# Hybrid attention and recurrence layer: query and key halves stored by 64 rows, the inverse written by lane group

## The chip, the cores and the metric

One core of a Trainium2 chip runs the whole layer as one program. The metric is the device time of one execution in microseconds (us). In what follows PE is TensorE (PEld its weight loads), DVE is VectorE, ACT is ScalarE, POOL is GpSimd and SP is SyncE, which in this program only issues DMAs. The core has 16 DMA engines, which all queues share. "Line 378" or L378 is a line of the kernel before.

## The reference

One layer of a diffusion backbone, for 1,024 latent tokens and 256 context tokens of width 1,024, in float32. One input projection feeds two groups of heads.

```
h = rmsnorm(x) * (1 + scale) + shift;  u = h @ w_in
q, k, v, g_a, u_b, g_b = split(u)
# A: 8 heads of differential attention (two softmaxes of 64 columns each, one subtracted
#    from the other); latent tokens get a 2-D rotary on q and k and also read 512 cached keys
o_a = rmsnorm((softmax(q1 k1) - lam * softmax(q2 k2)) v) * silu(g_a)
# B: 16 heads of a bidirectional RWKV-7 recurrence, state 64 x 64 per head and direction
S = S * w_t + (S @ -kk_t) b_t^T + v_t k_t^T;   y_t = S r_t
o_b = (groupnorm(y) + bonus) * silu(g_b)
x = x + gate * (concat(o_a, o_b) @ w_out);  y = rmsnorm(x)
```

Outputs are both token sets, the context tokens' keys and values, and the final states of the recurrence.

## The kernel before

The program has two phases. In **phase one** (to about 1,460 us) the input projection runs as a list of 66 blocks of 128 columns, each in three chunks of 512, 512 and 256 tokens (`chunk`, lines 336 to 338, PE). After each chunk ACT copies the result out of PSUM, and every block that is still in work (a Python generator in the list `active`) issues its next piece. So the pieces of several blocks are interleaved on the in-order queues of ACT, DVE, POOL and SP.

- `b_qk` (one block for the query, one for the key of each of the 8 attention heads) has the query or key of one head transposed, 128 rows by 1,280 tokens: rows 0 to 63 are the first half (m = 0), rows 64 to 127 the second. It applies the rotary, splits the result into a high part (`hi`, ACT, line 624 or 616) and a low part (left in `u`, DVE, line 625 or 617), and stores both to DRAM. For six of the heads `hi` is one buffer of 512 tokens that is used three times in a row; for the last two heads it is one of 1,280 tokens. The key's block does the same with 512 cached keys (`ch`, `ck`, lines 604 to 608). Everything is stored through SP.
- `b_k` prepares the recurrence of a pair of heads: decays (`z`, line 417), operands (DVE `ra`, `bk`; POOL `ta`, `bk`, lines 476 to 485), products (`pg`, line 451) masked by DVE into `km` (line 452), a single buffer that SP stores twice (`kt`, `bt`, lines 460 and 462).
- The last blocks of the list are those of heads 6 and 7 of attention. Their `u` tiles come from a pool of four buffers, so a new block's copy out of PSUM waits until an older block's store has read its buffer. Beside them POOL computes the first triangular inverse (`inverse`, lines 737 and 739: 31 pairs of multiply and add).

In **phase two** ("mix") the recurrence goes through 10 items (2 groups of heads, 5 token segments), each in 4 parts. Each part loads its operands (`load_part`), and two parts ahead `load_early` loads `Bt` and `Tb`; `Tb` is the part's share of the item's inverse, read back from the DRAM tile `td`. `prep` (line 806, `yb`) multiplies the two. Between the steps, attention (`sc`, `pb`, `pa`, `po`), the norms and the output projection are filled in by a credit count. POOL computes the inverse of a later item meanwhile and writes it to `td` through its own DMA queue (line 741); the next inverse begins with a memset of the same SBUF tile (`tt`, line 732).

The initial states of the recurrence are transposed by PE ahead of the first item (line 831) and written to DRAM; before and after do this in the same way.

The lines that say how the two layouts stand:

```
s["q"]: [H, HD, 2, 2, T]      # head, row of the half, high/low, half m, token
s["k"]: [H, 2, HD, 2, NK]     # head, high/low, row of the half, half m, token
dq = lambda v, c: (...).rearrange("r m t -> m r t")   # 2 x 64 x tokens, from 128 rows
td0 = dram.tile([CH, P, CH], F32)                     # t, lane, s
```

Of the kernel before, what the change touches and what calls it, by code (L numbers as in the profile page):

```python
# [10 lines left out]
F32 = mybir.dt.float32  # L11
# [7 lines left out]
P = 128  # L19
# [4 lines left out]
T = TL + TP  # L24
NT = T // P
PAST = 512
# [6 lines left out]
CH = 32  # L33
# [4 lines left out]
HN = 2  # L38
NF = NC // HN
NL = 4  # L40
# [43 lines left out]
def tile_kernel(ctx: ExitStack, tc: tile.TileContext, i: dict, o: dict, heads=H, phases=3):  # L84
    nc = tc.nc

    dram = ctx.enter_context(tc.tile_pool(name="dram", bufs=1, space=DRAM))
    kp = ctx.enter_context(tc.tile_pool(name="kp", bufs=1, reuse_waits="tile"))
    s = {}
# [19 lines left out]
    scratch("y", [heads // NL, T, 2, 2, NL // 2, P])  # L109
    scratch("acc", [T, D])  # L110
    gate_d = s["gate"]
    td0 = dram.tile([CH, P, CH], F32, tag="td0", name="td0")

    ident = kp.tile([P, P], F32, name="ident")
    nc.sync.dma_start(ident, i["ident"])
# [7 lines left out]
    with ExitStack() as p1:  # L123
# [5 lines left out]
        n = 0  # L129
# [4 lines left out]
        n = 128  # L134
# [37 lines left out]
        with ExitStack() as p0:  # L172
# [24 lines left out]
            for n, g in enumerate(WORD):  # L197
                t = sp.tile([P, KD, 256], F32, tag="wa", name=f"wa{g}", bufs=8)
# [143 lines left out]
        def ut(nm):  # L342
            return up.tile([P, UP], F32, tag="u", name=nm)

        def plain(u):
            def f(ps, n0, n):
                nc.scalar.copy(u[:, n0:n0 + n], ps)
            return f
# [28 lines left out]
        def spill(dst, t):  # L377
            nc.sync.dma_start(dst, t)  # L378
# [196 lines left out]
            spill(s[name][j * P:(j + 1) * P, :], g)  # L575

        def b_qk(which, h):
            dq = lambda v, c: (s["q"][h, :, v, :, c] if which == "q" else s["k"][h, v, :, :, c]).rearrange("r m t -> m r t")
            off = PAST if which == "k" else 0
            u = ut(f"u{which}{h}")  # L580
            yield plain(u)
            su = ut(f"su{which}{h}")
            for b in range(8):
                nc.sync.dma_start(su[16 * b:16 * b + 16, 0:TL], u[16 * (b ^ 1):16 * (b ^ 1) + 16, 0:TL])
            if which == "k":
                ck = ap.tile([P, PAST // P, P], F32, tag="w2", name=f"ck{h}")
                nc.sync.dma_start(ck, i["cache_k"][0, 0, :, h].rearrange("(t p) m d -> p t (m d)", p=P))
            yield
            yield
            nc.gpsimd.tensor_tensor(su[:, 0:TL], su[:, 0:TL], sinT, op=ALU.mult)  # L590
            nc.gpsimd.tensor_tensor(u[:, 0:TL], u[:, 0:TL], cosT, op=ALU.mult)
            if which == "k":
                pk = psm.tile([P, 512], F32, tag="psm", name=f"pk{h}")
                ko = ap.tile([P, 512], F32, tag="hi", name=f"ko{h}", bufs=1)
                for t in range(2):
                    nc.tensor.transpose(pk[:, t * P:(t + 1) * P], u[:, TL + t * P:TL + (t + 1) * P], ident)
                nc.scalar.copy(ko[:, 0:2 * P], pk[:, 0:2 * P])
                nc.sync.dma_start(o["new_k"][0, 0, :, h].rearrange("(t p) m d -> p t (m d)", p=P),
                                  ko[:, 0:2 * P].rearrange("p (t n) -> p t n", n=P))
                pt = psm.tile([P, 512], F32, tag="psm", name=f"pck{h}")  # L600
                for t in range(4):
                    nc.tensor.transpose(pt[:, t * P:(t + 1) * P], ck[:, t, :], ident)
                ch = ap.tile([P, 512], F32, tag="hi", name=f"ch{h}", bufs=1)
                nc.scalar.copy(ch.bitcast(F32R), pt)
                cv = ck.rearrange("p t n -> p (t n)")
                nc.vector.tensor_tensor(cv.bitcast(F32R), pt, ch, op=ALU.subtract)
                nc.sync.dma_start(dq(0, slice(0, PAST)), ch)
                nc.sync.dma_start(dq(1, slice(0, PAST)), cv)
            yield
            yield  # L610
            nc.vector.tensor_tensor(u[:, 0:TL], u[:, 0:TL], su[:, 0:TL], op=ALU.add)
            if h >= heads - 2:
                hi = up.tile([P, T], F32, tag="s", name=f"hi{which}{h}", bufs=3)
                for n0, n in CHUNKS:
                    c = slice(n0, n0 + n)
                    nc.scalar.copy(hi[:, c].bitcast(F32R), u[:, c])
                    nc.vector.tensor_tensor(u[:, c].bitcast(F32R), u[:, c], hi[:, c], op=ALU.subtract)
                yield
                spill(dq(0, slice(off, off + T)), hi)
                spill(dq(1, slice(off, off + T)), u[:, 0:T])  # L620
                return
            for n0, n in CHUNKS:
                hi = ap.tile([P, 512], F32, tag="hi", name=f"hi{which}{h}_{n0}", bufs=1)[:, :n]
                nc.scalar.copy(hi.bitcast(F32R), u[:, n0:n0 + n])
                nc.vector.tensor_tensor(u[:, n0:n0 + n].bitcast(F32R), u[:, n0:n0 + n], hi, op=ALU.subtract)
                spill(dq(0, slice(off + n0, off + n0 + n)), hi)
            spill(dq(1, slice(off, off + T)), u[:, 0:T])

        def b_va(h):
            u = ut(f"uv{h}")[:, 0:T]  # L630
# [33 lines left out]
        def b_inv():  # L664
            nw = heads * 10
            nc.sync.dma_start(s["wc"][:, 0:nw, :], wcs[:, 0:heads].rearrange("r p i d c -> r (p i d) c"))
            yield
            aw = rp.tile([P, T], F32, tag="td", name="aw0")[:, 0:CH * CH].rearrange("p (t y) -> p t y", y=CH)
            tt = rp.tile([P, T], F32, tag="ta", name="tt0")[:, 0:CH * CH].rearrange("p (t y) -> p t y", y=CH)
            tmp = rp.tile([P, T], F32, tag="kn", name="tmp0")  # L670
            for n, _ in enumerate(inverse(nc, s, td0, inv_rows(heads, 0), aw, tt, tmp)):
                if n % 8 == 0:
                    yield

        rk = lambda h: [(COL_R + h * P, b_r(h), f"r{h}"), (COL_KB + h * P, b_k(h), f"k{h}"),
                        (COL_VB + h * P, b_v(h), f"v{h}"), (COL_GB + h * P, b_gate("gb", h), f"gb{h}")]
        at = lambda h: [(COL_Q + h * P, b_qk("q", h), f"aq{h}"), (COL_K + h * P, b_qk("k", h), f"ak{h}"),
                        (COL_V + h * P, b_va(h), f"av{h}"), (COL_GA + h * P, b_gate("ga", h), f"ga{h}")]
        sr = [t for h in range(heads) for t in rk(h)]
# [5 lines left out]
        for n, t in enumerate(sr[3:]):  # L685
            m = round((n + 1) * (len(sa) - LAG) / (len(sr) - 3))
# [33 lines left out]
def inv_rows(heads, b):  # L720
    return [(NL * (b // 5) + x, b % 5 - 1) for x in range(NL)]


def inverse(nc, s, td, rows, aw, tt, tmp):
    n = 32 * len(rows)
    for x, (p, sg) in enumerate(rows):
        bt = s["bt"][p // NL, sg + 1, :, :, :, :, p % NL].rearrange("f h d t y -> (f h d) t y")
        for c in range(HN):
            nc.sync.dma_start(aw[NL * c + x:n:NL * HN], bt[:, :, c * P + 96:c * P + P])
    yield  # L730
    e = nc.gpsimd
    e.memset(tt[:n], 0.0)
    e.memset(tt.rearrange("p s t -> p (s t)")[:n, 0:CH * CH:CH + 1], 1.0)
    for t in range(CH - 1):
        j, w = t + 1, CH - 1 - t
        mv = tmp[:n, 0:j * w].rearrange("p (w j) -> p w j", w=w)
        e.tensor_tensor(mv, aw[:n, t, t + 1:CH].unsqueeze(2).broadcast_to([n, w, j]),  # L737
                        tt[:n, t:t + 1, 0:j].broadcast_to([n, w, j]), op=ALU.mult)
        e.tensor_tensor(tt[:n, t + 1:CH, 0:j], tt[:n, t + 1:CH, 0:j], mv, op=ALU.add)  # L739
        yield  # L740
    nc.gpsimd.dma_start(td[:, 0:n].rearrange("t u s -> u t s"), tt[:n])


def mix_phase(ctx, tc, i, o, s, ident, nhalf, dram, td0, neglam, subg, lnh, heads, psm):
    nc = tc.nc
# [38 lines left out]
    tds = {0: td0}  # L784
# [3 lines left out]
    def load_early(j):  # L788
        m, f = j // NF, j % NF
        p0, sg = items[m]  # L790
        Bt = cp.tile([P, NL, HN, P], F32, tag="Bt", name=f"Bt{j}")
        nc.sync.dma_start(Bt.rearrange("r x c y -> r (x c y)"),
                          s["bt"][p0 // NL, sg + 1, f].rearrange("h d r x y -> (h d r) (x y)"))
        Tb = cp.tile([P, HN, NL, CH], F32, tag="Tb", name=f"Tb{j}")
        src = tds[m].rearrange("t (f q u) s -> f q t (u s)", f=NF, q=4)
        nc.sync.dma_start(Tb.rearrange("t c x s -> t (c x s)"), src[f])
        early[j] = (Bt, Tb)

    def prep(j, w, pp, chain):
# [27 lines left out]
    for g in range(heads // NL):  # L827
        for d in range(2):
# [3 lines left out]
            c = 512 * (2 * g + d)  # L832
# [6 lines left out]
    for w in duos:  # L839
        yield  # L840
        pp = psm.tile([P, 512], F32, tag="psm", name=f"pp{w}")
        prep(0, w, pp, [])
        put(0, w, pp)
    load_early(1)
    yield True

# [11 lines left out]
    def invert(b):  # L858
        rows = inv_rows(heads, b)
        aw = wk.tile([P, CH, CH], F32, tag="aw", name=f"aw{b}")  # L860
        tt = wk.tile([P, CH, CH], F32, tag="tt", name=f"tt{b}")
        tmp = wk.tile([P, CH * CH // 4], F32, tag="tmp", name=f"tmp{b}")
        tds[b] = dram.tile([CH, P, CH], F32, tag=f"td{b % 2}", name=f"td{b}")
        yield from inverse(nc, s, tds[b], rows, aw, tt, tmp)

    bank = [psx.tile([P, 512], F32, name=f"bank{n}") for n in range(2)]
# [603 lines left out]
    for t in range(n_tick):  # L1470
        m, c = t // NC, t % NC
        p0, sg = items[m]
        j, k = t // HN, t % HN
# [120 lines left out]
```

## Time and profile before

| | |
|---|---|
| median of 3 runs | 2894.51 us (2891.80 to 2897.08) |
| the profiled execution | 2891.34 us, its span 2889.6 us |
| PE busy | 2402.2 us, 83% |
| DVE, ACT, POOL busy | 1424.4, 1218.8, 1120.2 us (49%, 42%, 39%) |
| DMA queue of SP | 510,000 packets, 429.24 MB, 59.1% of 16 engines' span |
| DMA queue of POOL | 1,840 packets, 5.49 MB, 1.0% |
| mean granted TensorE clock | 0.912 |

Busy times are those of the span. The span holds everything from the first to the last instruction; about 2 us of the execution lie around it. An engine's busy time says how much work it has, not that the end waits for it: what sets the end is read stage by stage, from which wait ends last there.

### The profile page before, as it was taken

Reading aid. Unit: us, or ns where it says so; the run is one execution under the profiler, and the core shown is the slowest. Engines: PE = TensorE matmul, PEld = TensorE weight load, DVE = VectorE, ACT = ScalarE, POOL = GpSimd, SP = SyncE. Lnnn points to the kernel's source line nnn. Section 1 sums busy time; section 2 is a strip of 40 time slices with the busy share of each in tenths; the row PEclk is TensorE's granted clock in tenths of the full one; section 3 lists DMA queues with packets and bytes.
Section 4 is the critical chain, followed back from the end, with each engine's and each line's share of the span. In section 5 each row is a group of like instructions: output and inputs, shape, how many; then the busy total and the mean of one; then the engine's idle time right before and its main releaser. Section 6 shows DMA issues by size and latency. Waiting matters only on the chain. (4 is left out here: it accounts for less than half of the span.)

```text
span 2889.6 us, 59844 instructions
## 1 busy us (share of the span) xinstructions
PE 2402.2 (83%) x23875; PEld 1931.3 (67%) x23875; DVE 1424.4 (49%) x2794; ACT 1218.8 (42%) x2518; POOL 1120.2 (39%) x1655
## 2 busy tenths in 40 slices
PE   6978779896887987986644689889989998998896
PEld 5766667775776866865543577767757767676674
DVE  5634353543534453542112467656665544446666
ACT  3323333332333332322113577756655656454343
POOL 4233243332333333332622667656662221105354
PEclk9998899997998999998877899999989999799898
DMA  7354545553543644554237988978687977857534
GB/s 235 99 131 105 157 115 134 141 128 98 148 118 94 158 111 125 143 124 122 73 93 187 194 192 195 201 146 186 144 191 182 232 169 177 195 162 211 165 129 164
DMA packets 512119, 438.55 MB, mean 152 GB/s; under 512 B 155719, under 2 KB 449779, under 8 KB 510496
## 3 DMA queue, kind: packets, MB, share of 16 engines
q1 hardware_dynamic: 510000, 429.24, 59.1%
q0 software_dynamic: 1840, 5.49, 1.0%
q8 instruction: 188, 3.08, 0.5%
q14 instruction: 91, 0.75, 0.1%
HBM read 259.22 MB, written 164.39 MB: 147 GB/s over the span
## 5 line engine op out<-in xcount | busy, mean ns | idle before, releaser
L1090 PE MATMUL sc<-ka,q 128*128 128x512 f32 (+1 forms) x832 | 297.5, 444 | 35.7 <-DVE pb L1093 19.3
L1093 DVE TENSOR_SCALAR_CACHE_REDUCE pb<-sc,mn 128x512 f32<-128x512 f32 x256 | 191.5, 748 | 131.3 <-PE sc L1090 116.7
L1098 ACT ACTIVATE pb<-pb,mn 128x1536 f32<-128x1536 f32 (+1 forms) x160 | 218.2, 1364 | 80.9 <-DVE pb L1093 79.4
L1135 PE MATMUL po<-vk,aT 128*128 128x128 f32 x1600 | 244.6, 291 | 6.0 <-ACT aT L1122 5.9
L458 ACT COPY km<-ptk 64x256 f32<-64x256 f32 x320 | 117.5, 367 | 288.3 <-PE ptk L455 169.9
L483 POOL TENSOR_SCALAR ta<-ta,ka 128x256 f32<-128x256 f32 x80 | 90.6, 1132 | 378.9 <-DVE bk L481 373.2
L1135 PEld LDWEIGHTS po<-vk,aT 128*128 128x128 f32 x1600 | 217.5, 200 | 29.7 <-ACT aT L1122 8.9
L451 PE MATMUL pg<-ra,bk 64*64 64x64 f32 x2560 | 101.8, 235 | 115.7 <-POOL bk L485 93.7
L737 POOL TENSOR_TENSOR tmp<-aw,tt 128x31 f32<-128x31 f32 (+15 forms) x310 | 162.2, 523 | 91.4 <-DMA aw<-bt 61.4
L1090 PEld LDWEIGHTS sc<-ka,q 128*128 128x128 f32 x832 | 139.3, 198 | 74.6 <-DVE pb L1093 33.1
L739 POOL TENSOR_TENSOR tt<-tt,tmp 128x31 f32<-128x31 f32 (+15 forms) x310 | 180.5, 582 | 18.4
L451 PEld LDWEIGHTS pg<-ra,bk 64*64 64x64 f32 x2560 | 90.3, 147 | 140.1 <-POOL bk L485 102.6
L452 DVE TENSOR_TENSOR km<-pg,msk 128x512 f32<-128x512 f32 x80 | 55.1, 689 | 247.3 <-PE pg L451 155.3
L812 ACT COPY L<-yb 32x384 f32<-32x384 f32 x312 | 146.6, 470 | 54.4 <-PE yb L806 50.7
L1120 PE MATMUL pa<-ident,pb 128*128 128x128 f32 x800 | 138.4, 291 | 32.4 <-ACT aT L1122 15.9
L1093 DVE TENSOR_SCALAR_CACHE_REDUCE pb<-sc 128x512 f32<-128x512 f32 (+1 forms) x160 | 101.1, 634 | 128.7 <-PE sc L1090 115.0
L1112 DVE SCALAR_TENSOR_TENSOR pb<-pb,cc,pb 128x512 f32<-128x512 f32 (+1 forms) x208 | 161.3, 822 | 2.0
L1327 POOL TENSOR_TENSOR olo<-of,ohi 128x512 fp32r<-128x512 f32 x30 | 38.3, 1278 | 292.1 <-ACT ohi L1326 228.1
L1122 ACT COPY aT<-pa 128x512 f32<-128x512 f32 (+1 forms) x208 | 115.7, 571 | 81.9 <-PE pa L1120 80.3
L1120 PEld LDWEIGHTS pa<-ident,pb 128*128 128x128 f32 x800 | 98.2, 146 | 63.9 <-ACT aT L1122 18.9
L806 PE MATMUL yb<-Bt,Tb 32*32 32x96 f32 x2496 | 110.2, 260 | 27.8 <-DMA Tb<-td 11.4
L931 ACT COPY R<-bank 32x256 f32<-32x256 f32 x320 | 116.2, 363 | 40.5 <-PE bank L923 36.4
(354 smaller groups left out, 6478.3 us busy)
## 6 DMA issues: line engine op xcount, KB each, us to landing
acc<-acc SPq DMA_DIRECT2D x50, 512.0 KB
ra<-ra SPq DMA_DIRECT2D x160, 128.0 KB
kt<-km SPq DMA_DIRECT2D x160, 128.0 KB
bt<-km SPq DMA_DIRECT2D x160, 128.0 KB
Bt<-bt SPq DMA_DIRECT2D x40, 512.0 KB
L<-kt SPq DMA_DIRECT2D x40, 512.0 KB
L<-ra SPq DMA_DIRECT2D x40, 512.0 KB
q<-q SPq DMA_DIRECT2D x32, 512.0 KB
```

The lines of the kernel that those rows point to most:

```text
L451: nc.tensor.matmul(pg[hs, c, :], bk[hs, c, :], ra[hs, c, :], start=True, stop=True)
L458: nc.scalar.copy(km[64 * h:64 * h + 64, e:NC:2, 0:HD], pt[64 * e:64 * e + 64, :, 64 * h:64 * h + 64])
L737: e.tensor_tensor(mv, aw[:n, t, t + 1:CH].unsqueeze(2).broadcast_to([n, w, j]), tt[:n, t:t + 1, 0:j].broadcast_to([n, w, j]), op=ALU.mult)
L739: e.tensor_tensor(tt[:n, t + 1:CH, 0:j], tt[:n, t + 1:CH, 0:j], mv, op=ALU.add)
L812: nc.scalar.copy(L[96:128, 2 * w:2 * w + 2, q // 2, q % 2, :, 0:96], pp[32 * q:32 * q + 32, 0:192 * HN].rearrange("p (e c y) -> p e c y", ...
L931: hold(nc.scalar.copy(R[96:128, k, :, 2 * w:2 * w + 2, hv(h)], bank[0][u:u + 32, 0:256].rearrange("p (d e v) -> p d e v", d=2, e=2)))
L1090: nc.tensor.matmul(sc, q[:, v, m, qc], ka[:, m, 0:kn], start=(v == 0), stop=(v == 1))
L1093: nc.vector.tensor_scalar(pm[:, c * 512:c * 512 + kn], sc, -0.125, mn[:, c - 1:c] if c else None, op0=ALU.mult, op1=ALU.min, accum_out=mn[ ...
L1098: soon.append(lambda: nc.scalar.activation(v, v, AF.Exp, bias=mn[:, c:c + 1], scale=-1.0, accum_out=B["l"][:, m, B["b"]:B["b"] + 1]))
L1112: nc.vector.scalar_tensor_tensor(a, B["p"][1][:, v], B["cc"], a, op0=ALU.mult, op1=ALU.add)
L1120: nc.tensor.transpose(pt[:, t * P:(t + 1) * P], B["p"][0][:, 512 * c + t * P:512 * c + (t + 1) * P], ident)
L1135: nc.tensor.matmul(po, B["aT"][c][:, t * P:(t + 1) * P], vk[:, t, :], start=(c == 0 and t == 0), stop=(c == last and t == nt - 1))
```

## The change

Two transfers are issued in another form; what is computed stays the same.

1. `dq`, which stored 128 rows as one transfer with the destination ordered half, row, token, becomes `halves`: two transfers of 64 rows, one for each half, each with the destination ordered row, token. That holds for all 72 such stores: for each of heads 0 to 5 four of the query and six of the key, for heads 6 and 7 two and four.
2. The DRAM tile of an inverse changes its layout from [t, lane, s] to [group of 8 lanes, t, lane in the group, s]. The write of 128 lanes, one transfer on POOL's queue, becomes eight, each of the 16 lanes that have one place in their groups. The read of a part's share (`Tb`, 128 rows of 1,024 bytes) becomes one contiguous run of DRAM instead of 4 blocks of 32 separate rows.

```
-    td0 = dram.tile([CH, P, CH], F32, tag="td0", name="td0")
+    td0 = dram.tile([4 * NF, CH, NL * HN, CH], F32, tag="td0", name="td0")
...
         def b_qk(which, h):
-            dq = lambda v, c: (s["q"][h, :, v, :, c] if which == "q" else s["k"][h, v, :, :, c]).rearrange("r m t -> m r t")
+            def halves(v, c, t):
+                dst = s["q"][h, :, v, :, c] if which == "q" else s["k"][h, v, :, :, c]
+                for m in range(2):
+                    spill(dst[:, m], t[64 * m:64 * m + 64])
...
-                nc.sync.dma_start(dq(0, slice(0, PAST)), ch)
-                nc.sync.dma_start(dq(1, slice(0, PAST)), cv)
+                halves(0, slice(0, PAST), ch)
+                halves(1, slice(0, PAST), cv)
...
-                spill(dq(0, slice(off, off + T)), hi)
-                spill(dq(1, slice(off, off + T)), u[:, 0:T])
+                halves(0, slice(off, off + T), hi)
+                halves(1, slice(off, off + T), u[:, 0:T])
...
-                spill(dq(0, slice(off + n0, off + n0 + n)), hi)
-            spill(dq(1, slice(off, off + T)), u[:, 0:T])
+                halves(0, slice(off + n0, off + n0 + n), hi)
+            halves(1, slice(off, off + T), u[:, 0:T])
...
-    nc.gpsimd.dma_start(td[:, 0:n].rearrange("t u s -> u t s"), tt[:n])
+    for x in range(NL * HN):
+        nc.gpsimd.dma_start(td[:, :, x], tt[x:n:NL * HN])
...
-        src = tds[m].rearrange("t (f q u) s -> f q t (u s)", f=NF, q=4)
-        nc.sync.dma_start(Tb.rearrange("t c x s -> t (c x s)"), src[f])
+        nc.sync.dma_start(Tb.rearrange("t c x s -> t (c x s)"), tds[m][4 * f:4 * f + 4].rearrange("q t u s -> (q t) (u s)"))
...
-        tds[b] = dram.tile([CH, P, CH], F32, tag=f"td{b % 2}", name=f"td{b}")
+        tds[b] = dram.tile([4 * NF, CH, NL * HN, CH], F32, tag=f"td{b % 2}", name=f"td{b}")
```

## Rows read from the trace of the kernel before

**Rows 1.** Windows by stage: length, each engine's busy time, granted clock, DMA share, GB/s.
```profile
130.00:1460.00 1330.00, 1080.80 (x8064) 910.27 (x8062) 561.06 (x886) 398.75 (x772) 434.75 (x484) 0.91 0.48 123
...
1640.00:2640.00 1000.00, 920.67 (x12643) 700.43 (x12641) 579.17 (x1321) 622.32 (x1353) 455.87 (x843) 0.94 0.80 183
```

**Rows 2.** Windows of the end of phase one, columns as above (PE, PEld, DVE, ACT, POOL).
```profile
1387.40:1497.40 110.00, 56.26 (x253) 46.48 (x252) 16.39 (x29) 11.20 (x22) 47.23 (x55) 0.75 0.25 73
...
1478.00:1490.00 12.00, 0.00 (x0) 0.00 (x0) 0.00 (x0) 0.00 (x0) 0.00 (x0) 0.63 0.13 52
```

**Rows 3.** Timeline of ACT there: start, length, instruction, idle time before and its releaser.
```profile
1417.37 0.59 ACT L347 COPY uk<-psg_ak 128x512 f32<-128x512 f32 x1 [29.95 <-issue]
...
1490.43 0.59 ACT L347 COPY uv<-psg_av 128x512 f32<-128x512 f32 x1 [27.03 <-DMA q<-uq]
```

**Rows 4.** Timeline of SP there: start and length of the issue.
```profile
1418.46 0.51 SPq L607 DMA_DIRECT2D k<-ch  x1
...
1431.72 0.55 SPq L378 DMA_DIRECT2D k<-hik  x1
...
1462.60 0.56 SPq L378 DMA_DIRECT2D q<-hiq  x1
```

**Rows 5.** Waits from 130 to 1,460 us: waiter, releaser: total us, times, longest us.
```profile
ACT hik L624 <- DMA k<-hik: 94.5, 12, 11.3
...
PE pg L451 <- POOL bk L485: 93.7, 24, 16.5
DVE km L452 <- DMA bt<-km: 92.0, 10, 17.9
...
ACT hiq L624 <- DMA q<-hiq: 81.5, 12, 8.7
...
PE z L417 <- DVE km L452: 55.5, 6, 12.1
...
ACT hik L624 <- DMA k<-ch: 49.1, 6, 10.8
...
PE pgt L650 <- DMA w_ada<-w_ada: 13.6, 1, 13.6
```

**Rows 6.** Timelines of ACT and PE around 515 us.
```profile
514.29 0.40 ACT L624 CAST hik<-uk 128x256 fp32r<-128x256 f32 x1 [8.07 <-DMA k<-hik]
...
515.81 0.58 PE L417 MATMUL z<-los,w2h 128*128 128x256 f32 x1 [12.10 <-DVE km L452]
```

**Rows 7.** Timelines of SP, POOL and DVE, 168 to 179 us: two other kinds of store.
```profile
168.64 0.53 SPq L378 DMA_DIRECT2D bv<-s_v  x1
...
173.00 2.52 POOL L590 TENSOR_TENSOR suq<-suq,sinT 128x1024 f32<-128x1024 f32 x1 [4.77 <-DMA bv<-s_v]
...
175.11 1.31 SPq L479 DMA_DIRECT2D ra<-ra  x2
...
178.10 1.23 DVE L611 TENSOR_TENSOR uq<-uq,suq 128x1024 f32<-128x1024 f32 x1 [2.30 <-DMA ra<-ra]
```

**Rows 8.** Timelines of ACT and PE at the start of phase two.
```profile
1547.52 1.08 ACT L362 ACTIVATE ga<-psg_ga 128x512 f32<-128x512 f32 x2 [23.88 <-DMA k<-uk]
...
1549.53 1.08 PE L923 MATMUL bank<-R,L 96*32 96x64 f32 x32 [17.26 <-issue]
```

**Rows 9.** DMA issues on POOL's queue: count, KB each, median us to landing.
```profile
td<-tt POOLq DMA_DIRECT2D x10, 512.0 KB, 9.5
...
vst<-lnx_b POOLq DMA_DIRECT2D x1, 4.0 KB, 5.2
```

**Rows 10.** Tiles td, vst, Tb: ns min/median/max, first and last start; a wait of Tb.
```profile
L741 POOL DMA_DIRECT2D td<-tt x10: 1741/1791/1824, 1497.3 to 2157.8; - x10
...
L216 POOL DMA_DIRECT2D vst<-lnx_b x1: 521/521/521, 6.2 to 6.2; - x1
...
L796 SPq DMA_DIRECT2D Tb<-td x40: 542/556/2282, 1510.9 to 2528.8; - x40
...
  DMA Tb<-td: 22.1, 7
```

## The prediction

> **What bounds the kernel now.** I read the windows by stage first, then who ended whose waits in phase one, then the timelines of its end, then the DMA views. In phase one PE is busy 1,080.8 of 1,330 us and no other engine is busy half of the time [rows 1], so the stage is bound by PE wherever it isn't waiting; in the middle of phase two PE is busy 920.7 of 1,000 us and the DMA engines 0.80 of the time, POOL 455.9 us [rows 1]. What PE loses, it loses in phase one and around its end.
>
> There the timelines show what the losses are. From 1,478 to 1,490 us no engine does anything, while the DMA engines are busy 0.13 of the time and move 52 GB/s [rows 2]: 0.13 x 16 is two engines. What is under way is the pair of 640 KB stores (high and low part of a query) of which the first was issued at 1,462.60 us [rows 4]; ACT waits for a `u` buffer until 1,490.43 us [rows 3]: 27.8 us for a pair. Another store of 640 KB, `bv`, was issued at 168.64 us and had let POOL go at 173.00 us: 4.4 us [rows 7]. Two stores of 64 rows and 128 KB each (`ra`) were issued from 175.11 us on, and DVE, which waited for them, went on at 178.10 us: 3.0 us for 256 KB in two halves, 88 GB/s [rows 7]. So a store of 64 rows isn't held to 52 GB/s, and it is the form that the change gives the query and the key. The Trainium skill has the reason (DMA: Bandwidth & Descriptors, Rules for kernel authors): an outermost dimension below 16 confines a DMA to that many engines, and the half is such a dimension, of size 2. By that rule the new stores would spread over all 16; the 0.13 agrees.
>
> In the middle of phase one the same stores are 256 KB, into one `hi` buffer. ACT waits 94.5, 81.5 and 49.1 us for them in 30 waits, 7.5 us each [rows 5]. What is queued behind the waiting instruction on ACT are the copies out of PSUM and of `km`, on DVE the low parts and the mask, then POOL's operands, then PE: ACT waited 8.07 us for `k<-hik` until 514.29 us, and PE, idle for 12.10 us, went on at 515.81 us, after DVE's `km` [rows 6].
>
> **The change part by part, against the profiled execution of 2891.3 us.**
>
> *End of phase one.* Three pairs of 640 KB are waited for like the one above; the first and the last end ACT's idle times of 29.95 and 27.03 us [rows 3]. A pair after the change: 4.4 us for the first 640 KB [rows 7], and for the second the data time between the 3.0 us of 256 KB and the 4.4 us of 640 KB, 1.4 us for 384 KB, so 2.4 us for 640 KB; together 6.8, and with four issues of 0.55 us [rows 4] up to 9; I take 8. That frees 3 x (27.8 - 8) = 59 us. The two stores of cached keys hold SP from 1,418.46 to 1,431.72 us [rows 4], 13.3 us, which should be 5: 8 more, 67 in all. What is late next is PE's own work: of the 110 us from 1,387.4 to 1,497.4 PE is busy 56.3 and POOL 47.2 [rows 2], so no more than 54 us can go unless PE's clock, 0.75 here, rises too. I take **50**; ends 35 and 60.
>
> *Middle of phase one.* Each of ACT's 30 waits falls from 7.5 us to at most the 3.0 us of `ra` [rows 7], less what passes between issue and wait; I take 2.3 us, so 225 - 69 = 156 us come off ACT. What of it reaches PE, I take from PE's waits [rows 5]: 55.5 us in six waits on `km`, which lies behind the low part on DVE or waits for `bt<-km`, a store that is itself queued behind the stores on two engines (92.0 us in ten waits, 9.2 us each, for 128 KB); at the 2.3 us of a quiet store 6 x 2.3 = 14 stay and 42 go. The 13.6 us on `w_ada`, a load issued behind a store pair: all, 13. Of the 93.7 us in 24 waits on POOL's `bk`, a third, 31, since most are short (3.9 us in the mean) and POOL's own chain stays. Together 86; a fifth goes to whatever is late next, 69 are left, and the granted clock of 0.91 [rows 1] gives some 11 us back when the gaps before it falls are gone: **80**. Ends: 25, if half of the `km` waits alone go, and 115 of the 163 us of these three kinds of wait.
>
> *Start of phase two.* ACT waits 23.88 us for the last low part of the key (`k<-uk`, one store of 640 KB), and the first step of the recurrence comes 17.26 us late on PE, just after it [rows 8]. At 4.4 us instead of some 18 the step comes 13 us earlier; the loads before it lose their queue too, **16** in all; ends 8 and 25.
>
> *`Tb`.* Forty loads, on which PE and its weight loads wait 22.1 us in 7 waits [rows 10]; the two engines wait at the same time, so 11 us on the path. A contiguous read can take away at most that: **4**; ends 0 and 11.
>
> *Eight writes on POOL.* One write of 512 KB costs POOL 1.79 us of issue [rows 10] and lands in 9.5 us [rows 9]. A small one (4 KB) costs 0.52 us [rows 10]; one eighth of the elements lies between, 0.52 + 1.27/8 = 0.68 us, so eight cost 5.4 instead of 1.8 us. They land while the next ones are issued: the small ones land in 5.2 us at an issue of 0.52 us each [rows 9, 10]. The last lands at about 0.68 x 7 + 5.2 = 10 us instead of 9.5. The cover is that POOL works on a later item's inverse and is busy 46% of the stage [rows 1]; the first two inverses have no lead and pay it themselves: **-2**. Ends: +4, and -28 if eight issues take 1.79 us each (14.3 + 9.5 against 9.5, twice).
>
> *SP.* 72 more issues at 0.5 us, 37 us of SP's time over phase one, and behind them weight loads and `km` stores; SP spends most of a pair's time waiting now: **-3**; ends 0 and -10.
>
> Sum: 50 + 80 + 16 + 4 - 2 - 3 = 145 us, 2891.3 - 145 = 2746; the median of the runs is 3 us above the profiled one: **2749 us**. All lower ends together give 30 us (2864), all upper ones 219 (2676).
>
> **The rivals.** *A: the middle of phase one gives little.* The waits on ACT go, but PE is then held by the next link, POOL's operands, of whose 93.7 us nothing shows a store by name. Then it gives 10 to 20 us and not 80: 50 + 16 + 4 + 15 - 5 = 80, about 2815 (2790 to 2860). Against it: POOL is busy only 435 of 1,330 us and has the room to catch up [rows 1].
>
> *B: the halves don't spread.* Two halves that ran one after the other at the rate of one whole would land at the same time as before, and the issues would be left: 72 x 0.5 us, of which some 5 lie on the path: 2899 (2885 to 2905). The Trainium skill speaks for this one (the same section): splitting a transfer into two on disjoint partition halves brings nothing, since both halves use the same 16 engines and go one after the other; by it the change would cost just its issues. The 52 GB/s of the whole against the 88 GB/s of two halves speaks against it [rows 2, 7]: what this rule takes for granted, all 16 engines for the whole, doesn't hold here.
>
> *C: slower, by the eight writes.* If each lands only when the one before it has, an inverse is written in 8 x 9.5 = 76 us, 66 more than now. POOL now makes an inverse every (2157.8 - 1497.3)/9 = 73 us and the recurrence takes an item every (2528.8 - 1510.9) x 4/39 = 104 us [rows 10]. POOL would then set the pace at 140 us: 66 + 9 x 36 = 390 us lost against 147 won, some 3135. It decides from 42 us more per inverse on, 42 + 9 x (42 - 31) = 141, where 6.5 us per write would do. Against it stand the small writes: issued every 0.52 us, landed in 5.2 us each.
>
> **How the numbers follow.** My forecast, that the stores are on the path in all of phase one: 0.75, with a range of its own of 2690 to 2790. A 0.17, B 0.05, C 0.03. What a measurement of this kernel can tell from no change is about 0.2%, 6 us. Faster: the forecast and A, and a little of B, 0.93; same: 0.03, of B; slower: 0.04, C and the rest of B. The range reaches to the middle of A and stops short of the sum of all upper ends: 2690 to 2825.
>
> **What would show it.** In the profile after, ACT's waits on `hik` and `hiq` stores should fall from 225 to under 80 us in all, the window in which nothing but a DMA share of 0.13 is left should be gone, and phase one's end, seen in the first `td` write at 1,497 us, should come 110 to 140 us earlier. The middle of phase two should keep its length within 15 us, the 80 `td` writes should take 0.5 to 0.8 us each and the waits for `Tb` be shorter. If the first write moves by only 60 us, it is A; if the pairs still take 27 us, B; if a memset of `tt` waits for 60 us, C. The prediction would also be wrong if the order of instructions on the engines, which is made anew for the changed program, put other waits in place of these.

## The result and the profile after

The changed kernel takes 2592.86 us, median of 4 runs (2582.28 to 2599.56), against 2893.16 us for the kernel before on the same chip: a ratio of 0.896, 95% interval 0.892 to 0.899. That is 300 us less, twice the 145 us of the forecast and outside its range. The profiled execution took 2582.28 us with a span of 2580.5 us, 309 us less than the span before, and its windows say where they went. The cuts are the first memset of `tt`, the first write to `td`, the first step of the recurrence (`bank`) and the end; the columns are those of [rows 1]. First the kernel before, cut at these events:

```profile
130.00:1361.80 1231.80, 1021.23 (x7738) 859.86 (x7737) 548.26 (x872) 386.63 (x748) 386.96 (x430) 0.92 0.49 126
1361.80:1497.30 135.50, 81.76 (x419) 68.56 (x418) 21.46 (x33) 18.70 (x37) 64.48 (x77) 0.80 0.30 79
1497.30:1549.50 52.20, 27.05 (x208) 22.17 (x206) 10.72 (x34) 9.53 (x20) 4.48 (x5) 0.80 0.71 164
1549.50:2889.60 1340.10, 1170.65 (x14544) 898.88 (x14544) 770.76 (x1742) 757.87 (x1639) 618.41 (x1070) 0.92 0.75 180
```

Then the changed kernel, cut at the same events:

```profile
130.00:1133.00 1003.00, 974.96 (x7733) 823.69 (x7732) 560.21 (x870) 388.48 (x746) 389.27 (x429) 0.99 0.62 155
1133.00:1210.30 77.30, 77.30 (x436) 66.67 (x435) 26.72 (x37) 18.88 (x36) 65.64 (x78) 1.00 0.62 145
1210.30:1243.30 33.00, 22.65 (x191) 18.93 (x189) 8.83 (x29) 9.35 (x20) 7.59 (x12) 0.92 0.97 222
1243.30:2580.50 1337.20, 1185.57 (x14544) 903.09 (x14544) 786.96 (x1742) 758.91 (x1639) 660.75 (x1133) 0.92 0.74 181
```

The four stretches give 229, 58, 19 and 3 us, together the 309. In the first, PE's idle time (length less its busy time) falls from 211 to 28 us, and its busy time for the same matmuls from 1,021 to 975 us: the granted clock rises from 0.92 to 0.99. In the second PE is never idle. The DMA engines have about as much to do as before (0.49 x 1,231.8 = 604 us and 0.62 x 1,003 = 622 us on each), in less time.

Of the waits of [rows 5] these are left from 130 to 1,133 us (total us, times, longest):

```profile
ACT hiq L628 <- DMA q<-hiq: 27.2, 9, 6.1
...
ACT hik L628 <- DMA k<-hik: 23.2, 9, 5.2
...
PE pg L451 <- POOL bk L485: 20.3, 13, 4.8
...
ACT hik L628 <- DMA k<-ch: 18.1, 6, 5.2
...
PE z L417 <- DVE km L452: 0.3, 1, 0.3
```

ACT's three kinds of wait have fallen from 225 to 68.5 us, 2.9 us each. PE's wait on `km` is gone, and what is left of that on POOL's `bk` is about a fifth.

A fourth wait of ACT, as long in all as the longest of [rows 5], isn't among those rows: its copy into `km` waits for the store of the last `km`. Before (130 to 1,361.8 us), then in the changed kernel:

```profile
ACT km L458 <- DMA bt<-km: 94.4, 8, 19.5
```

```profile
ACT km L458 <- DMA bt<-km: 3.8, 1, 3.8
```

The standstill of [rows 2, 3, 4] is gone too. The timelines of SP and of ACT of the changed kernel at the same pair of stores:

```profile
1191.63 1.18 SPq L378 DMA_DIRECT2D q<-hiq  x2
1192.91 2.20 SPq L378 DMA_DIRECT2D q<-uq  x2
```

```profile
1199.07 0.59 ACT L347 COPY uv<-psg_av 128x512 f32<-128x512 f32 x1 [9.87 <-issue]
```

Four issues go out within 3.5 us, and ACT's copy follows 7.4 us after the first of them, with no DMA as its releaser. PE is busy all through. How long one half of 320 KB takes from issue to landing is in the DMA issues (count, KB, median us): 3.6 us.

```profile
q<-uq SPq DMA_DIRECT2D x16, 320.0 KB, 3.6
```

The memsets of `tt` and the writes of `td`, first by tile (ns min/median/max, first and last start), then by the DMA issues (count, KB, median us to landing):

```profile
L736 POOL MEMSET tt<- x10: 951/954/971, 1132.8 to 1820.9; 128x1024 f32 x10
L746 POOL DMA_DIRECT2D td<-tt x80: 622/622/745, 1210.3 to 1898.7; - x80
```

```profile
td<-tt POOLq DMA_DIRECT2D x80, 64.0 KB, 4.3
```

One of the eight writes takes POOL 0.62 us and lands in 4.3 us; the one before took 1.79 and landed in 9.5 us [rows 9, 10].

### The profile page after: what moved, and what is told of

It reads as the page before. It is cut to its first block, busy times and chain, and to the rows that moved or that the text cites. A ratio compares the mean times of both kernels' runs of the same rounds, so it can differ in the third digit from the quotient of the medians.

```text
span 2580.5 us, 60062 instructions
## 1 busy us (share of the span) xinstructions
PE 2361.8 (92%) x23875; PEld 1894.0 (73%) x23875; DVE 1457.1 (56%) x2794; ACT 1222.2 (47%) x2518; POOL 1169.3 (45%) x1725
## 5 line engine op out<-in xcount | busy, mean ns | idle before, releaser
L1094 PE MATMUL sc<-ka,q 128*128 128x512 f32 (+1 forms) x832 | 303.2, 455 | 34.3 <-DVE pb L1097 22.2
L743 POOL TENSOR_TENSOR tt<-tt,tmp 128x31 f32<-128x31 f32 (+15 forms) x310 | 186.5, 602 | 21.1
L1116 DVE SCALAR_TENSOR_TENSOR pb<-pb,cc,pb 128x512 f32<-128x512 f32 (+1 forms) x208 | 170.5, 866 | 2.0
L810 PE MATMUL yb<-Bt,Tb 32*32 32x96 f32 x2496 | 116.3, 259 | 27.5 <-DMA Tb<-td 18.6
L962 DVE TENSOR_TENSOR R<-bank,wc 64x512 f32<-64x512 f32 x152 | 104.3, 686 | 47.1 <-PE bank L948 46.1
L948 PEld LDWEIGHTS bank<-R,L 128*64 128x64 f32 x2560 | 93.6, 145 | 37.1 <-issue 18.8
```

What stands on the lines that cost most here:

```text
L810: follow(nc.tensor.matmul(pp[g, n:n + 96], Tb[g, c, 2 * w + e, :], Bt[g, 2 * w + e, c, 0:96], start=True, stop=True, tile_position=(32 * q ...
L948: x = nc.tensor.matmul(bank[1][hv(h), o_:o_ + 64], L[:, x_, h, d, k, 0:64], R[:, k, d, x_, hv(h)], start=True, stop=True, tile_position=(0 ...
L1094: nc.tensor.matmul(sc, q[:, v, m, qc], ka[:, m, 0:kn], start=(v == 0), stop=(v == 1))
L1116: nc.vector.scalar_tensor_tensor(a, B["p"][1][:, v], B["cc"], a, op0=ALU.mult, op1=ALU.add)
```

## The experiments

All ratios are to the kernel before on the same chip, whose medians lay between 2891 and 2898 us. Two theories of where 300 us come from were set against each other. **Direct waits** (theory 1): ACT waits for its own stores, since `hi` is one buffer, and hands the delay on. **Backlog** (theory 2): a store on two engines holds up what SP issues behind it (`km` stores, weight loads, loads of operands), whoever waits for that.

### The two parts of the change alone

The first leaves out the `td` edits; the second is the kernel before with these edits alone.

```
# e1_halves_only                     # e2_td_only
 halves(...)  as changed              dq(...)  as before
 td0, write, Tb read  as before       td0, eight writes, Tb read  as changed
```

> The change's first part alone: the 72 query and key stores in halves of 64 rows, the inverse written and read as before. Theory (the two-engine stores are all of it): within 8 us of the whole change, so 2585 to 2605 us, and the first write of an inverse near 1210 us. Rival (the new layout of the inverse carries a part that the prediction put at 2 us): 2620 us or more.

> The change's second part alone: eight writes and a contiguous read of the inverse, query and key stored whole. Theory: no change that can be told, 2885 to 2900 us; POOL's 80 issues take 0.62 us each as in the changed kernel. Rival: 2870 us or less, if the waits for Tb were worth their 11 us and more.

The halves alone: 2616.32 us, ratio 0.903 (0.900 to 0.907). The `td` edits alone: 2883.59 us, 0.997 (0.995 to 1.000). So 278 of the 300 us belong to the stores. That is 11 us short of what was expected if they were all of it. By the first step of the recurrence the halves alone have won 300 us (1,549.5 to 1,249.4 us), but their phase two is 26 us longer than before (1,365.7 against 1,340.1). The rest is larger beside the halves (0.9032 to 0.8957, some 22 us) than alone (some 8 us by the ratio); the last group of runs takes that up.

### Which stores: the middle or the end

```
+                if not (h < 6):      # e4_last_two_heads: h >= 6
+                    spill(dst.rearrange("r m t -> m r t"), t)
+                    return
                 for m in range(2):
                     spill(dst[:, m], t[64 * m:64 * m + 64])
```

`td` is as before in both.

> Halves for the query and key of heads 0 to 5 only; heads 6 and 7 stored whole, the inverse as before. The first memset of the inverse's tile, which came at 1362 us before and at 1133 us in the changed kernel, marks the end of the middle of phase one. Theory (the middle of phase one alone was worth 229 us): the memset at 1133 to 1160 us, the time 2655 to 2680 us, and from the memset to the first write still 135 us. Rival (the middle gave 80 us as predicted, and the rest comes from an order of instructions that fits better): about 2800 us.

> Halves for heads 6 and 7 only; heads 0 to 5 stored whole. Theory: the first memset stays within 20 us of 1362 us, the stretch from it to the first write falls from 135 to about 77 us and that to the first step from 52 to about 33 us: 2805 to 2825 us. Rival (the end of phase one is worth less by itself, because the inverse on POOL sets it): 2850 us.

Heads 0 to 5 give 0.925 (0.923 to 0.927), 2674 us; heads 6 and 7 give 0.980 (0.978 to 0.982), 2834 us; 7.5% and 2.0% add up to e1's 9.7% within the intervals. The tiles show the two places apart, `tt` and `td` first in the kernel with heads 0 to 5 in halves, then in the one with heads 6 and 7:

```profile
L739 POOL MEMSET tt<- x10: 946/947/970, 1138.2 to 1871.3; 128x1024 f32 x10
...
L748 POOL DMA_DIRECT2D td<-tt x10: 1738/1791/1932, 1272.9 to 1943.9; - x10
```

```profile
L739 POOL MEMSET tt<- x10: 946/952/970, 1358.2 to 2043.7; 128x1024 f32 x10
...
L748 POOL DMA_DIRECT2D td<-tt x10: 1738/1794/1824, 1436.4 to 2105.8; - x10
```

With heads 0 to 5 the memset comes 224 us earlier and the first inverse still takes 135 us; with heads 6 and 7 the memset comes 4 us earlier and the inverse takes 78 us. The unexpected size lies in the middle of phase one, not at its end. The time with heads 6 and 7 is 9 us above the 2805 to 2825 us expected: the first step comes 77 us earlier (at 1,472.7 us), but phase two is 27 us longer than before (1,367.5 us).

### Direct waits or backlog: the high or the low parts alone

```
-                if not (h < 6):
+                if not (v == 0):     # e5_high_only;  v == 1: e6_low_only
```

The high parts are what ACT's single buffer waits for. The low part stands in one of four `u` buffers, and little in the middle waits for its store by name (25 us in four waits before).

> Halves for the high parts alone (the stores whose buffer ACT waits for); the low parts, in heads 0 to 5 the 640 KB that nobody waits for at once, stay whole, the inverse as before. Theory 1 (the prediction's: ACT's direct waits for the high buffer are the loss): the first memset of the inverse's tile, at 1362 us before and at 1138 us with the first six heads in halves, comes at 1150 to 1190 us; 2690 us or less. Theory 2 (the backlog of the two engines holds up everything that is issued behind a whole store, whoever it belongs to): the low parts are half of the bytes, so about half of the 224 us stays: memset at 1230 to 1290 us, 2740 to 2790 us.

> The other way round: halves for the low parts alone, the high parts stay whole. Theory 1: ACT's 30 waits stay at 7 us and more each, and so does most of the loss: memset at 1310 us or later, 2820 us or more. Theory 2: memset at 1220 to 1290 us, 2740 to 2790 us, and ACT's waits on the high stores get shorter by themselves, since nothing is queued ahead of them.

Each gives half: 2756 us, 0.952 (0.948 to 0.955), and 2758 us, 0.952 (0.948 to 0.956). The first memset comes at 1,257.9 and 1,265.9 us, 104 and 96 us earlier. ACT's waits from 130 to 1,460 us, with the high parts in halves, then with the low ones:

```profile
ACT km L458 <- DMA bt<-km: 78.9, 6, 18.2
...
ACT hik L631 <- DMA k<-hik: 32.4, 11, 7.0
ACT hiq L631 <- DMA q<-hiq: 27.2, 9, 6.3
...
ACT hik L631 <- DMA k<-ch: 19.3, 6, 5.3
```

```profile
ACT hiq L631 <- DMA q<-hiq: 84.3, 12, 8.8
ACT hik L631 <- DMA k<-hik: 79.4, 12, 8.1
ACT hik L631 <- DMA k<-ch: 47.7, 6, 10.2
...
ACT km L458 <- DMA bt<-km: 30.3, 5, 10.7
```

In the first the direct waits are down from 225 to 78.9 us, and ACT still waits for `bt<-km`, a store of 128 KB: by chance also 78.9 us, of 94.4 before, up to 18.2 us at a time. In the second 211 of the 225 us of direct waits are still there, those for `bt<-km` have fallen from 94.4 to 30.3 us, and half of the gain has come. Both times and both memsets lie where theory 2 expected them, and outside what theory 1 expected. So direct waits can't be all of it: the low parts are worth as much as the high ones. How the half of the high parts divides between ACT's direct waits and what stands behind the stores, no run separates; the waits (146 us off the direct ones, 16 off those for `bt<-km`) speak for the direct ones. Theory 2 missed one thing: ACT's own waits hardly shortened in the second.

### The backlog by itself

To have stores on two engines for which no engine waits, the gate of attention (8 stores of 640 KB in phase one, in the changed kernel whole tiles to contiguous rows) is given the old form of the query.

```
-    scratch("ga", [D, T])
+    scratch("ga", [H, HD, 2, T])          # e13: [H, 32, 4, T]
...
+            if name == "ga":
+                spill(s["ga"][j].rearrange("r m t -> m r t"), g)
+                # e10: for m in range(2): spill(s["ga"][j][:, m], g[64 * m:64 * m + 64])
+                return
...
-            nc.sync.dma_start(ga, s["ga"][h * P:(h + 1) * P, c])
+            for m in range(2):             # e13: four of 32 rows
+                nc.sync.dma_start(ga[64 * m:64 * m + 64], s["ga"][h, :, m, c])
```

The second kernel is the control: the same tile and loads, but the store in halves. The third has four blocks of 32 rows in one store.

> The changed kernel with one thing taken the other way: the attention gate's 8 stores of 640 KB (128 rows), which nobody waits for at once, go out whole to a DRAM tile whose order is half, row, token, so with an outer dimension of 2; its loads in phase two are split into two of 64 rows. Theory 2 (backlog): 8 stores x about 13 us of two engines; before, some 25 MB of whole stores cost 300 us, so 5.2 MB cost 30 to 70 us: 2620 to 2660 us, most of it ahead of the first write of an inverse (1210 us). Theory 1 (direct waits only): within 10 us of the changed kernel, 2585 to 2605 us.

> The control of the gate stored whole: the same DRAM tile and the same split loads, but the 8 gate stores as halves of 64 rows. Theory (backlog of two engines): back to within 12 us of the changed kernel, 2585 to 2605 us, first memset of the inverse's tile near 1133 us against 1180 us with the gate whole. Rival (the split loads or the tile's layout made the difference): 2635 to 2655 us again.

> As the gate stored whole, but in a DRAM tile with four groups of 32 rows, so the store's outer dimension is 4 in place of 2 (loads in four transfers of 32 rows). If the outer dimension sets the number of engines, each of the 8 stores occupies its engines half as long, and the first memset comes at 1140 to 1160 us (1133 with none, 1180 with two engines): 2600 to 2630 us. If any store that isn't a plain run of rows is slow, 2640 us or more.

Measured: two blocks 2648.92 us, 0.915 (0.912 to 0.918); control 2593.05 us, 0.896 (0.892 to 0.900); four blocks 2598.74 us, 0.900 (0.894 to 0.905). Eight stores in the form with two blocks cost 56 us against the control. The first memsets of `tt`, and ACT's waits for the store `bt<-km`, in the order two blocks, control, four blocks:

```profile
L739 POOL MEMSET tt<- x10: 942/953/971, 1179.9 to 1868.6; 128x1024 f32 x10
...
ACT km L458 <- DMA bt<-km: 82.4, 9, 14.6
```

```profile
L740 POOL MEMSET tt<- x10: 942/952/971, 1136.9 to 1813.2; 128x1024 f32 x10
...
ACT km L458 <- DMA bt<-km: 9.5, 2, 5.5
```

```profile
L739 POOL MEMSET tt<- x10: 948/952/972, 1151.3 to 1839.1; 128x1024 f32 x10
...
ACT km L458 <- DMA bt<-km: 50.4, 9, 10.8
```

Against the control the memset comes 43 us later with two blocks and 14 with four, and the wait grows from 9.5 to 82.4 and 50.4 us. The victim is a store of another tensor on the same queue. SP's timeline shows where the delay sits. Behind the first gate store (issued at about 305 us in all three) come two or three short issues and then a `kt` store; its issue (start, length), in the same order:

```profile
308.73 10.31 SPq L460 DMA_DIRECT2D kt<-km  x1
```

```profile
309.03 1.30 SPq L460 DMA_DIRECT2D kt<-km  x1
```

```profile
307.68 6.04 SPq L460 DMA_DIRECT2D kt<-km  x1
```

SP itself spends 10.31 us in that issue with two blocks, 6.04 with four and 1.30 in the control, and whatever it would issue next comes later by that much. With this the backlog is shown and not only argued, and it grows as the outer dimension shrinks. In total four blocks aren't told apart from the control. Phase two is 14 us longer than the control's with two blocks and 18 shorter with four (1,357.7 and 1,326.5 against 1,344.0 us), which the backlog of phase one doesn't explain; so of the 56 us it is shown to cost the 43.

### What an issue costs

```
                 for m in range(2):
-                    spill(dst[:, m], t[64 * m:64 * m + 64])
+                    for r in range(0, 64, 32):
+                        spill(dst[r:r + 32, m], t[64 * m + r:64 * m + r + 32])
```

`td` is as before, so the comparison is with the halves alone.

> As the run with halves alone, but each half in two transfers of 32 rows, so 144 more issues than halves. Theory (an issue of some 0.5 us on SP costs next to nothing, and a transfer of 32 rows spreads as well as one of 64): within 12 us of the halves alone, 2605 to 2630 us. Rival (SP's issues are now what phase one waits for): 144 x 0.5 = 72 us more of SP and 20 to 70 us more in all.

It takes 2627.74 us, 0.908 (0.903 to 0.913), against 2616.32 us and 0.903. The intervals meet; the memset comes at 1,149.6 us against 1,135.0. By these medians and memsets 144 more issues cost 11 to 15 us, some 0.1 us each on the path, and the 72 that the change adds around 7. Since the intervals meet, that is an estimate and not a shown price.

### The second part: write or read

All have the halves. The first keeps the old layout and the one write, and reads `Tb` in four transfers of 32 rows; the second keeps the old layout and the one read, and writes by eight.

```
# e11_read_by_four
-        nc.sync.dma_start(Tb.rearrange("t c x s -> t (c x s)"), src[f])
+        for q in range(4):
+            nc.sync.dma_start(Tb[32 * q:32 * q + 32].rearrange("t c x s -> t (c x s)"), src[f, q])
# e12_write_by_eight
+    for x in range(NL * HN):
+        nc.gpsimd.dma_start(td[:, x:n:NL * HN].rearrange("t u s -> u t s"), tt[x:n:NL * HN])
```

> Halves, the inverse written as before, but Tb read by four transfers of 32 rows each instead of one transfer of 4 x 32 rows. The run with halves alone took 2616 us, the whole change 2593. Theory (the second part gains by the read, whose 4 x 32 rows go over four engines and lie behind other loads): 2590 to 2605 us. Rival (by the eight writes, or by the order of the instructions): 2612 to 2625 us.

> Halves, Tb read as before, but the inverse written in eight transfers of 16 lanes into the old layout. Theory (the read gains): within 10 us of the halves alone, 2608 to 2628 us. Rival (the writes gain): 2600 us or less.

The read by four takes 2576.71 us, 0.890 (0.886 to 0.894), the writes by eight 2601.65 us, 0.899 (0.895 to 0.904), the halves alone 0.903. The kernel with the read by four has the whole gain and more; the writes' own share isn't told apart from nothing, and their time lies between its two expectations. So four kernels were run on one chip: the changed one, the read by four, the changed one with the second half stored first (`for m in (1, 0)`), and the old layout with the read by four and the writes by eight.

> The changed kernel itself, on the chip of the three others: 2585 to 2600 us by every theory; it is what they are compared with.

> Halves, the inverse written by one transfer into the old layout, Tb read by four transfers of 32 rows. If the read is what the second part gains by: no slower than the changed kernel, 2565 to 2600 us. If the order made the 2577 us of its first run: it keeps its order, so it stays there too, and the next two runs decide.

> The changed kernel with the second half of each pair stored before the first. Nothing else differs. If the order of the instructions moves the time by itself, as phase two's lengths of 1327 to 1358 us among kernels with the same phase two suggest, it lies 8 to 20 us off the changed kernel, either way. If order is worth little: within 6 us.

> Halves, the inverse written by eight transfers into the old layout, Tb read by four. If the writes gain something of their own beside the read: 2560 to 2570 us. If they cost their 3.2 us of issue and no more: within 10 us of the read by four. If only the order decides: anywhere from 2565 to 2605 us.

Medians: 2586.44, 2578.48, 2585.18 and 2579.12 us; ratios 0.894, 0.890, 0.893 and 0.890, each within 0.004. All five runs of the read by four (2577.0 to 2580.5 us) lie below all five of the changed kernel (2583.3 to 2601.4). The version that beats both kernels is therefore the halves with the old layout, its one write, and the read by four: 8 us below the changed kernel. The eight writes add nothing to it, and the order of the halves, which was expected to move the time by 8 to 20 us if order matters by itself, nothing that can be measured.

Why the second part gave 2 us of phase two alone is in the windows of that phase, from the first step to the end: the `td` edits alone, the halves alone, and the read by four in its second run and in its first:

```profile
1547.30:2885.80 1338.50, 1188.26 (x14544) 904.67 (x14544) 786.18 (x1742) 758.64 (x1639) 659.02 (x1133) 0.92 0.73 180
```

```profile
1249.40:2615.10 1365.70, 1203.94 (x14544) 914.89 (x14544) 780.52 (x1742) 757.92 (x1639) 627.44 (x1070) 0.90 0.73 177
```

```profile
1252.40:2578.70 1326.30, 1165.58 (x14544) 894.04 (x14544) 778.22 (x1741) 756.80 (x1639) 623.23 (x1070) 0.93 0.75 182
```

```profile
1252.20:2576.80 1324.60, 1176.20 (x14544) 902.63 (x14544) 778.80 (x1741) 757.60 (x1639) 624.76 (x1070) 0.92 0.75 183
```

With the `td` edits alone PE's idle time falls from 169 us before (1340.1 - 1170.7) to 150, and PE's busy time for the same 14,544 matmuls rises from 1,171 to 1,188. The halves alone and the second run of the read by four differ by 39 us in length and by 38 in PE's busy time, with clocks of 0.90 and 0.93, while both leave PE idle for 161 to 162 us. But the last two lines are one and the same kernel: at nearly the same length its PE is idle for 161 us in one execution and for 148 in the other, and busy for 1,166 and 1,176. Parts of some 12 us can therefore not be read from one profile of each kernel; the 38 us of busy time are more than that. PE's waits for `Tb` don't follow the form of the read either: PE and its weight loads wait 22.1 us before, 44.6 with the halves alone, 19.6 in the changed kernel, 39.5 and 30.2 in the two runs of the read by four, and 15.5 with the writes by eight, whose read is that of before. What sets the rate of the same matmuls from one kernel to the next, the runs leave open, and with it how much of the 8 us is the read's own.

## Why the prediction was wrong

The direction and the mechanism were right: stores of 64 rows are not held to 52 GB/s, and they were on the path in all of phase one. The size was wrong, in one term above all.

**Middle of phase one: 80 us forecast, 229 measured.** This step failed. Its upper end was 115. Five of its choices were too low:

- PE's waits on POOL's `bk` were credited at a third, "since most are short (3.9 us in the mean) and POOL's own chain stays". They fell from 93.7 to 20.3 us, and to 18.6 with the halves alone, where nothing but stores differs: most of their length came from waits on stores further up. The name of the last releaser hid the first; the links between weren't traced one by one.
- What would come off ACT was put at 156 us, from the three kinds of wait in [rows 5]. Its waits for `bt<-km` weren't counted, and 90.6 us came off them too (94.4 to 3.8).
- Only three kinds of PE's waits were counted, 163 us. PE was idle for 211. Before, it also waited 22.0 us for DVE's `bk`, 12.5 for ACT's `w2h` and 10.1 for `km` in another place; of these 2.2 us is left, in the wait for `bk`.
- "A fifth goes to whatever is late next": little was. PE's idle time is 28 us, 20.3 of it the wait on `bk`.
- The clock was to give back some 11 us, for which the prediction shows no working; PE's busy time fell by 46.

183 us of idle time and 46 of faster matmuls make the 229. The experiments show that the stores of high and of low parts weigh the same. The forecast started from ACT's direct waits on the high ones, and of the backlog it credited only what reached PE through the `km` stores and `w_ada`.

**End of phase one: 50 forecast, 58 measured** (135.5 to 77.3 us), inside its bounds. The cap, PE's own work at a clock of 0.75, was put as one that only a rising clock could lift; it rose to 1.00.

**Start of phase two: 16 forecast, 19 measured** (52.2 to 33.0 us). ACT's wait there is 14 us and no longer 24, and its releaser another store.

**Phase two: `Tb` 4, the eight writes -2; measured 3 in all.** The sum fits here by luck: in the profiles of before and of the `td` edits alone the second part took 19 us off PE's idle time, and slower matmuls took 18 back, parts hardly larger than the 12 us between two executions of one kernel. One write took POOL 0.62 us (0.68 forecast) and landed in 4.3 us, so rival C's serial landing didn't come; POOL's memsets of `tt`, which waited 54.1 us for `td` before, waited 3.1 us.

**SP: -3 forecast.** By the quarters an estimated -7, not told apart from nothing.

**The sums.** The prediction's upper ends add up to 215 us (60 + 115 + 25 + 11 + 4 + 0) and not 219, so that bound is 2679 and not 2676; nothing else hangs on it.

**The rivals.** A, that POOL's operands would hold PE, is refuted by the 20.3 us. B, that the halves run one after the other at the old rate, by the halves of 320 KB that land in 3.6 us and by the time. The rule that spoke for B, the Trainium skill's (DMA: Bandwidth & Descriptors, Rules for kernel authors) that splitting over disjoint partition halves brings nothing, is contradicted by e1 in this form of store: the split alone took 278 us off. The rule of the same section that a small outermost dimension confines a transfer to at most as many engines agrees with the stores with two blocks, at a DMA share of 0.13 [rows 2], or 2/16, and with those with four blocks, which cost phase one a third of what two did (14 and 43 us).

The signs that the prediction named: ACT's waits under 80 us came (68.5), the empty window went, the `td` writes and phase two's length fitted, but the waits for `Tb` didn't clearly get shorter: 22.1 to 19.6 us for PE and its weight loads together, 11.4 to 18.6 for PE alone. The first `td` write was to move by 110 to 140 us and moved by 287; that sign alone told that the term of the middle was too small.

## What to carry to other kernels

Look for stretches in which all engines stand still and the DMA share stays at a small, constant fraction: here 0.13, or 2/16, pointed to a transfer on two engines, and its form (a small outer dimension of the destination) is worth changing before any schedule. Its price isn't only the wait that names it: what the queue holds behind it, and short waits further down the chain in the same stage, can belong to it, so the bound is the stage's whole idle time of PE plus what a higher clock gives back on its busy time (here 211 and 46 us). Read the idle time first and divide it among causes afterwards. Here waits put down to POOL, which was busy for a third of the stage, were mostly waits on something further up. Look at the issuing engine too: here an issue of 10 us, where others of the same store take 0.4, stood behind such a transfer.

## What was not expected of the hardware

- A transfer on few engines delays transfers behind it on the queue that have nothing to do with it: eight stores of 640 KB with an outer dimension of 2 cost 43 us by the first memset of `tt`; with 4 it was 14 us. SP was held for 10.31 us in one issue behind such a store, 1.30 in the control.
- On top of the 183 us of stalls the faster matmuls gave a quarter as much again: with the stalls gone from the middle of phase one, the same matmuls took 975 us at a clock of 0.99 and not 1,021 at 0.92. In phase two the same 14,544 matmuls took between 1,166 and 1,204 us in kernels that don't differ there in their PE work, and 1,166 and 1,176 in two executions of one kernel.
- POOL's issue of a `td` write fell from 1.79 to 0.62 us when it had 64 instead of 512 KB, and an eighth of the pieces, close to the 0.52 us of one of 4 KB [rows 10]: most of the price of the large one grew with its size.
